# A two-layer attention and mixture-of-experts kernel: grouped column tiles, paired output products, shared reciprocals, contiguous weight pieces, more warming products

## The chip, the cores and the metric

One core of one Trainium2 chip runs the whole program. The metric is device time in microseconds (us) of that core for one execution; smaller is better. In this text PE is TensorE (matrix products), DVE is VectorE, ACT is ScalarE, POOL is GpSimd and SP is SyncE, which issues nearly all loads.

## What is computed

256 tokens of width 1024 go through two layers, all in float32. Cut to what matters:

```python
for i in range(2):
    xn = rms_norm(h, ln_mix[i])
    mix = nsa_attention(xn, ...) if i == 0 else moba_attention(xn, kb, vb, km, ...)
    h = h + mix                                   # 16 heads of 64, output projection 1024x1024
    h = h + hier_moe(rms_norm(h, ln_ffn[i]), ...) # 32 experts, 2 of them for each token
    gate = sigmoid(rms_norm(h, ln_ple[i]) @ ple_w_gate[i])
    h = h + gate * (p[i] @ ple_w_proj[i])

# nsa_attention: o = g0 * softmax(compressed) @ vc + g1 * softmax(selected) @ vs + g2 * softmax(window) @ vw
# hier_moe: hid = silu(x @ w_gate[e]) * (x @ w_up[e]); y = sum_e cw[e] * (hid @ w_down[e])
```

An expert has gate and up weights of 1024x128 each (1 MB together) and a down weight of 128x1024 (512 KB).

## The kernel before

Every product with a dense weight is made of three faster ones: a value is split into a high and a low half (ACT writes the high half, DVE the rest), and high times high, high times low and low times high are summed (L351 to L353, helper `mm3`). `Weights` (L109 to L132) loads a weight in pieces of two 128-row blocks and splits each block into a tile `wsp`; `xT` is the transposed input, loaded in between. The first such weight is B_c. Ahead of it `keep_warm` (L148, called at L599) lets PE multiply ones by ones eight times.

Attention runs over eight steps c, two heads each (`attend`, L500): scores of step c+1, the turn of step c (PE transposes the probabilities p0 and p1, L455 to L457), the softmax of step c+1, the products with the values (L473). In `softmax` (L416) DVE reduces, ACT takes the exponential with its sum, DVE takes the reciprocal (L434) and, in layer 0, multiplies it with the gate (L436), once for each head; then POOL scales the short tile p0 (L442, layer 0) and DVE the long tile p1 (L440). In layer 0 there are two branches (nbr is 2), in layer 1 one. The output projection is spread over the steps (`Out`, L529 to L557): the table ADD_AT names the step at which each piece j is multiplied, and DVE adds each result into the residual h (L540). Piece 3 comes in a tail. `Embedding.step` (L575) puts two further groups of products at steps 1 and 2.

In the mixture of experts, each expert takes up to 32 tokens. Four experts are one group j, and there are eight groups (L1287 to L1318). PE has four column tiles of 32 columns: products with `tile_position=(0, 32 * i)` go to tile i, for expert i of the group. `gate_up(j)` (L1170) makes eight steps k of four products of 128x256 (L1177); `hidden(j)` is ACT (L819, L821) and DVE (L822, L823) work on the result; `down(j)` (L1203) turns the hidden tile on PE (L1207), copies it (`hT`, L78), multiplies it with the down weights in two halves n of four products of 128x512 (L1221), splits each half (L340) and scatters the rows to their tokens (L1214). A ninth group holds one extra expert (`gate_up(8)`, L1183), whose weights POOL fetches by indirect transfers. `gate_up(j + 1)` and `hidden(j + 1)` are written ahead of `down(j)`. After the experts come L276 (transposes) and the products with ple_gate.

All loads stand on the queue of SP, in order, and go into a ring of SBUF, so a load starts when the tile that held its place is no longer used. A scheduler sets the order of the instructions of each engine from the code's order and its own estimates of when things are ready; it may put one product of a later group into a gap. Each engine then runs its list in order.

Of the kernel before, what the change touches and what calls it, by code (L numbers as in the profile page):

```python
# [18 lines left out]
P = 128  # L19
S = 256  # L20
# [19 lines left out]
def hybrid_kernel(ctx: ExitStack, tc: tile.TileContext, I: dict, out: bass.AP, dbg=None):  # L40
# [68 lines left out]
    class Weights:  # L109


        def __init__(self, w, g, turned=None):
            self.n, self.g, self.t, self.behind = w.shape[2], g, {}, []
# [302 lines left out]
    def softmax(c, nbr, raw, gates=None):  # L416

        a, i = divmod(c, 4)
        ws = []
        for b in range(2):  # L420
# [4 lines left out]
            mx = st("mx", [P, NT, nbr], bufs=4)  # L425
            sums = st("sums", [P, NT, nbr], bufs=4)
# [17 lines left out]
            ws.append((p0, p1))  # L444
# [55 lines left out]
    def attend(fill, after, nbr, qs, k1, k2, V, oT, gates=None, cmp=None):  # L500
# [3 lines left out]
        for c in range(8):  # L504
# [7 lines left out]
            if c < 7:  # L512
# [5 lines left out]
    ADD_AT = ((((3, 2), (3, 3)), ((4, 4), (4, 5)), ((7, 6), (7, 6))),  # L518
              (((3, 2), (3, 3)), ((5, 4), (5, 4)), ((6, 7), (7, 7))))

    class Out:
# [7 lines left out]
        def add(self, j, t, n):  # L529
            pt = pa([P, 512])  # L530
            for i in range(2):
                if self.l == 0:
                    w = self.w[j, i, n]
                    m = mm3(pt, [self.oT[j // 2][:, x, 2 * (j % 2) + i, t * P:(t + 1) * P] for x in range(2)],
                            [w[:, x] for x in range(2)], i == 0, i == 1)
                    continue
                m = nc.tensor.matmul(pt, self.oT[0][:, 2 * j + i, t * P:(t + 1) * P],  # L537
                                     self.raw[j][:, i, n * 512:(n + 1) * 512], start=(i == 0), stop=(i == 1))
# [10 lines left out]
        def step(self, c):  # L549
# [3 lines left out]
            for j in range(3):  # L553
                for t in range(NT):
                    for n in range(2):
                        if self.add_at[j][t][n] == c:
                            self.add(j, t, n)  # L557
# [3 lines left out]
    class Embedding:  # L561
# [13 lines left out]
        def step(self, c):  # L575
            if c in (1, 2):
                for n in range(2):
                    self.piece(c - 1, n)
# [20 lines left out]
    keep_warm(pts[0], 8)  # L599
# [226 lines left out]
    def moe(l, out_proj_tail, prefetch):  # L826
# [343 lines left out]
        def gate_up(j):  # L1170
            gu = pb([P, 3, P])
            xg = slots(j)
            if j < 8:
                wgu = wgus.pop(j)
# [335 lines left out]
```

## Time and profile before

| | |
|---|---|
| median of three timed runs | 553.49 us (550.83 to 555.04) |
| the profiled execution's own time | 546.59 us |
| its span in the trace | 544.8 us |
| PE busy | 518.6 us (95% of the span) |
| DVE, ACT, POOL busy | 341.0, 278.7, 51.9 us |
| loads | 147.16 MB, mean 270 GB/s |

Durations below are from the one profiled execution; 1.8 us of its time lie outside the span. A busy PE is not a PE at its peak: two products in two column tiles at once count like one that runs alone.

### The profile page before, as it was taken

The numbers are of one execution on the slowest core, as the hardware profiler recorded it, in microseconds if no ns is written. First come the engines' busy times: TensorE is split into PE (matmuls) and PEld (weight loads), VectorE is DVE, ScalarE is ACT, GpSimd is POOL, SyncE is SP. The second block draws the span as 40 slices with busy tenths as digits, with TensorE's granted clock in tenths as the row PEclk, the third lists the DMA queues.
The fourth block names the chain that finished last, engine by engine and source line by source line (L and its number), as shares of the span: only waits on it lengthen the run. The fifth ranks groups of instructions, "written<-read, shape, count | busy, mean of one in ns | idle before, by whom it ended". The sixth has DMA issues, their size and how long they took to land. (4 is left out here: it accounts for less than half of the span.)

```text
span 544.8 us, 10203 instructions
## 1 busy us (share of the span) xinstructions
PE 518.6 (95%) x3782; PEld 364.3 (67%) x3782; DVE 341.0 (63%) x1038; ACT 278.7 (51%) x650; POOL 51.9 (10%) x120
## 2 busy tenths in 40 slices
PE   6989999999998999999999999999997999899996
PEld 4968899578667766464448999755566655554386
DVE  4669978989966844323258975776748534142484
ACT  5729837976744242222349965763342413132491
POOL 5000402314330003100000000000000012000000
PEclk9999999999999899999999999999999999999999
DMA  8968650044779699999953678742555999999602
GB/s 288 426 244 306 225 225 2 1 155 152 300 284 333 217 426 416 410 417 416 400 231 117 220 275 374 295 149 98 192 206 221 385 420 418 417 417 401 247 1 77
DMA packets 32213, 147.16 MB, mean 270 GB/s; under 512 B 4000, under 2 KB 4272, under 8 KB 22304
## 3 DMA queue, kind: packets, MB, share of 16 engines
q1 hardware_dynamic: 31232, 144.39, 68.2%
q0 software_dynamic: 784, 2.05, 1.0%
q8 instruction: 31, 0.51, 0.4%
q14 instruction: 22, 0.18, 0.1%
q10 hardware_dynamic: 144, 0.04, 0.0%
HBM read 146.98 MB, written 1.05 MB: 272 GB/s over the span
## 5 line engine op out<-in xcount | busy, mean ns | idle before, releaser
L131 DVE SCALAR_TENSOR_TENSOR wsp<-raw,vec,wsp 128x512 fp32r<-128x512 f32 (+1 forms) x96 | 67.4, 747 | 5.5 <-ACT wsp L130 5.3
L130 ACT ACTIVATE wsp<-raw,vec 128x512 fp32r<-128x512 f32 (+1 forms) x96 | 62.6, 719 | 2.8 <-DMA raw<-in_w_c_dram 2.1
L1177 PE MATMUL pb<-wgu,X 128*32 128x256 f32 x768 | 56.9, 381 | 0.9 <-PEq L1295 0.6
L431 ACT ACTIVATE p<-p,mx 128x128 f32<-128x128 f32 (+1 forms) x96 | 42.5, 445 | 7.9 <-DVE mx L429 7.6
L819 ACT ACTIVATE p<-pb,srs 128x128 f32<-128x128 f32 x16 | 5.9, 367 | 77.0 <-PE pb L1177 70.0
L1177 PEld LDWEIGHTS pb<-wgu,X 128*32 128x32 f32 x768 | 29.9, 110 | 19.7 <-issue 3.4
L1221 PE MATMUL pb<-wd,hT 128*32 128x512 f32 x224 | 42.0, 595 | 0.7 <-issue 0.4
L351 PE MATMUL pa<-XA,wsp 128*128 128x256 f32 x128 | 38.3, 299 | 4.0 <-ACT wsp L130 3.3
L340 DVE TENSOR_TENSOR pta<-pb,p 128x512 fp32r<-128x512 f32 (+1 forms) x36 | 24.8, 690 | 24.4 <-ACT p L340 23.0
L353 PE MATMUL pa<-XA,wsp 128*128 128x256 f32 x128 | 37.2, 292 | 2.0 <-DVE wsp L131 2.0
L340 ACT CAST p<-pb 128x512 fp32r<-128x512 f32 (+1 forms) x36 | 21.0, 585 | 33.4 <-PE pb L1221 33.2
L352 PE MATMUL pa<-XB,wsp 128*128 128x256 f32 x128 | 37.3, 291 | 0.0
L822 DVE TENSOR_TENSOR p<-pb,ptb 128x128 f32<-128x128 f32 (+1 forms) x18 | 5.2, 289 | 43.3 <-ACT ptb L821 41.2
L442 POOL TENSOR_SCALAR p<-p,cf 128x128 f32<-128x128 f32 x32 | 25.6, 811 | 67.8 <-DVE cf L436 40.1
L460 ACT COPY pta<-pa 128x512 f32<-128x512 f32 (+1 forms) x32 | 14.6, 479 | 32.4 <-PE pa L456 32.4
L429 DVE CUSTOM_DVE_ANT_0 p<-pb,d_q 128x128 f32<-128x128 f32 (+1 forms) x96 | 29.4, 350 | 1.3 <-PE pa L455 0.9
L537 PE MATMUL pa<-wo,XH 128*128 128x512 f32 x64 | 29.4, 602 | 0.0
L351 PEld LDWEIGHTS pa<-XA,wsp 128*128 128x128 f32 x128 | 25.3, 198 | 5.9 <-ACT wsp L130 4.2
L1017 PE MATMUL pb<-rs,X 128*128 128x256 f32 (+1 forms) x192 | 27.1, 293 | 0.3 <-DVE X L1043 0.3
L1214 PE MATMUL pa<-p,rrow 128*128 128x512 f32 (+1 forms) x72 | 27.1, 424 | 0.2 <-ACT p L340 0.2
L1017 PEld LDWEIGHTS pb<-rs,X 128*128 128x128 f32 x192 | 24.3, 188 | 3.9 <-issue 1.2
L353 PEld LDWEIGHTS pa<-XA,wsp 128*128 128x128 f32 x128 | 25.1, 197 | 2.4 <-DVE wsp L131 2.4
(369 smaller groups left out, 1352.6 us busy)
## 6 DMA issues: line engine op xcount, KB each, us to landing
wgu<-in_moe_gu_dram SPq DMA_DIRECT2D x48, 1024.0 KB, 11.2
wd<-in_moe_w_down_dram SPq DMA_DIRECT2D x48, 512.0 KB, 9.8
wo<-in_w_out_dram SPq DMA_DIRECT2D x8, 1024.0 KB, 4.8
raw<-in_ple_gate_dram SPq DMA_DIRECT2D x16, 512.0 KB, 8.4
raw<-in_a_q_dram SPq DMA_DIRECT2D x8, 512.0 KB, 9.1
wd<-in_moe_w_down_dram SPq DMA_DIRECT2D x16, 256.0 KB, 7.8
XB<-in_moe_gu_dram SPq DMA_DIRECT2D x4, 1024.0 KB, 4.7
XA<-in_moe_gu_dram SPq DMA_DIRECT2D x4, 1024.0 KB, 4.9
```

What stands on the lines that cost most here:

```text
L130: nc.scalar.activation(hi, src, AF.Copy, scale=g)
L131: nc.vector.scalar_tensor_tensor(lo, src, g, hi.bitcast(F32), ALU.mult, ALU.subtract)
L340: return nc.scalar.copy(hi, src), eng.tensor_tensor(lo, src, hi.bitcast(F32), ALU.subtract)
L351: nc.tensor.matmul(o, a[0], b[0], start=first, stop=False)
L352: nc.tensor.matmul(o, a[0], b[1], start=False, stop=False)
L353: return nc.tensor.matmul(o, a[1], b[0], start=False, stop=last)
L429: nc.vector.tensor_tensor_reduce(pt_[:, br, :], st_[:, br, :], dt_, -SLOPE[hh], 3e38, ALU.add, ALU.min, accum_out=mx[:, t, br:br + 1])
L431: mark["exp", c] = nc.scalar.activation(pt_[:, br, :], pt_[:, br, :], AF.Exp, bias=mx[:, t, br:br + 1], scale=-1.0, accum_out=sums[:, t, b ...
L537: m = nc.tensor.matmul(pt, self.oT[0][:, 2 * j + i, t * P:(t + 1) * P], self.raw[j][:, i, n * 512:(n + 1) * 512], start=(i == 0), stop=(i ...
L1017: nc.tensor.matmul(pt, part_columns(x, t)[:, k, :], Gs[i][:, t, 0:e1], start=(t == x == 0), stop=(t == x == 1))
L1177: last_ = nc.tensor.matmul(gu[32 * i:32 * i + 32, 0:2], xg[:, k, 32 * i:32 * i + 32], wgu[i][k], start=(k == 0), stop=(k == NK - 1), tile_ ...
L1221: nc.tensor.matmul(ysp[32 * i:32 * i + 32, :], hT[:, 32 * i:32 * i + 32], wd[i][n], start=True, stop=True, tile_position=(0, 32 * i))
```

## The change

- `keep_warm` makes 18 products where it made 8.
- The pieces of weights and of xT lie contiguous in DRAM, where their rows lay apart. Bytes and transfers stay the same.
- In layer 0 the output products of pieces 0 and 1 are summed in one group of twelve products for each of four results, at steps 4 and 5, and added to h once; before, piece 0 was multiplied at step 3 and piece 1 at steps 4 and 5, with an addition each. There are 12 additions where there were 16.
- The second group of Embedding products moves from step 2 to step 3.
- Softmax takes one reciprocal (and in layer 0 one product with the gates) for both heads, and scales both heads' tiles behind it.
- In `gate_up` and `down` the experts of a group go from the last-loaded to the first, each product kept behind the one before it, so that the four column tiles stay together.

```diff
-                xT.append(load([P, 2, S], lambda t: [(t, turned[:, k:k + 2])], "xT"))
-            self.raw.append(load([P, 2, self.n], lambda t: [(t, w[:, k:k + 2])], "raw"))
+                xT.append(load([P, 2, S], lambda t: [(t, turned[k // 2])], "xT"))
+            self.raw.append(load([P, 2, self.n], lambda t: [(t, w[k // 2])], "raw"))
...
-            cf = st("cf", [P, NT, nbr], bufs=4)
-            nc.vector.reciprocal(cf, sums)
-            if gates is not None:
-                nc.vector.tensor_tensor(cf, cf, gates[:, :, 3 * hh + 1:3 * hh + 3], ALU.mult)
+            ws.append((p0, p1))
+        nc.vector.reciprocal(cfs, sums_)
+        if gates is not None:
+            g = gates.rearrange("p t (a b i j) -> p a b i t j", a=2, b=2, i=4)[:, a, :, i, :, 1:3]
+            nc.vector.tensor_tensor(cfs, cfs, g, ALU.mult)
+        for b in range(2):
+            p0, p1 = ws[b]
+            cf = cfs[:, b]
             for t, pt_ in enumerate((p0, p1)):
...
-    ADD_AT = ((((3, 2), (3, 3)), ((4, 4), (4, 5)), ((7, 6), (7, 6))),
-              (((3, 2), (3, 3)), ((5, 4), (5, 4)), ((6, 7), (7, 7))))
+    ADD_AT = ((((0, 1), ((4, 4), (5, 5))), (2, ((7, 6), (7, 6)))),
+              ((0, ((3, 2), (3, 3))), (1, ((5, 4), (5, 4))), (2, ((6, 7), (7, 7)))))
...
-            if c in (1, 2):
+            if c in (1, 3):
...
-    keep_warm(pts[0], 8)
+    keep_warm(pts[0], 18)
...
-                    for i in range(4):
-                        last_ = nc.tensor.matmul(gu[32 * i:32 * i + 32, 0:2], xg[:, k, 32 * i:32 * i + 32],
+                    for i in reversed(range(4)):
+                        with ExitStack() as es:
+                            if last_ is not None:
+                                es.enter_context(tc.issue_after(last_.ins))
+                            last_ = nc.tensor.matmul(gu[32 * i:32 * i + 32, 0:2], xg[:, k, 32 * i:32 * i + 32],
...
-                for i in range(m // 32):
-                    nc.tensor.matmul(ysp[32 * i:32 * i + 32, :], hT[:, 32 * i:32 * i + 32],
+                for i in reversed(range(m // 32)):
+                    with ExitStack() as es:
+                        if behind:
+                            es.enter_context(tc.issue_after(behind[0]))
+                        behind[:] = [nc.tensor.matmul(ysp[32 * i:32 * i + 32, :], hT[:, 32 * i:32 * i + 32],
```

What this does to PE's list, at three places of layer 0. Lines of the changed kernel are shifted: L1177 is L1189 there, L1183 is L1195, L1207 is L1219, L1214 is L1226, L1221 is L1238, L1017 is L1025. In a row, the tile written stands ahead of the arrow.

Place one, PE before, the scatter of the first group (pta and p are the low and high halves of its rows, wgu a gate and up weight of a later group):

```order
L1214 MATMUL pa_2265<-p_482_2508,rrow_2501 128x512
L1214 MATMUL pa_2267<-p_482_2508,rrow_2501 128x512
L1177 MATMUL pb_2545<-wgu_2365,X_467_2424 32x256
L1214 MATMUL pa_2265<-pta_2509,rrow_2501 128x512
L1214 MATMUL pa_2267<-pta_2509,rrow_2501 128x512
L1214 MATMUL pa_2266<-p_485_2517,rrow_2501 128x512
L1214 MATMUL pa_2266<-pta_2518,rrow_2501 128x512
L1214 MATMUL pa_2268<-p_485_2517,rrow_2501 128x512
```

The same place after the change:

```order
L1226 MATMUL pa_2227<-p_454_2470,rrow_2463 128x512
L1226 MATMUL pa_2229<-p_454_2470,rrow_2463 128x512
L1189 MATMUL pb_2507<-wgu_2333,X_439_2386 32x256
L1189 MATMUL pb_2507<-wgu_2331,X_439_2386 32x256
L1189 MATMUL pb_2507<-wgu_2329,X_439_2386 32x256
L1189 MATMUL pb_2507<-wgu_2327,X_439_2386 32x256
L1226 MATMUL pa_2227<-pta_2471,rrow_2463 128x512
L1226 MATMUL pa_2229<-pta_2471,rrow_2463 128x512
L1226 MATMUL pa_2228<-p_457_2479,rrow_2463 128x512
```

Before, one product of the next gate_up stands alone in the gap between the scatters of the high and the low half; after, all four column tiles of a step stand there.

Place two, PE before, from the end of gate_up(6) through down(5) (wd are down weights, hT the turned tile of group 5, pb_3068 the result of gate_up(6), which L1207 turns):

```order
L1177 MATMUL pb_3068<-wgu_2868,X_573_2934 32x256
L1221 MATMUL pb_3113<-wd_2870,hT_3109 32x512
L1221 MATMUL pb_3113<-wd_2872,hT_3109 32x512
L1221 MATMUL pb_3122<-wd_2870,hT_3109 32x512
L1221 MATMUL pb_3113<-wd_2874,hT_3109 32x512
L1221 MATMUL pb_3122<-wd_2872,hT_3109 32x512
L1221 MATMUL pb_3122<-wd_2874,hT_3109 32x512
L1207 MATMUL pb_3068<-ident,p_608_3103 128x128
L1221 MATMUL pb_3113<-wd_2876,hT_3109 32x512
L1221 MATMUL pb_3122<-wd_2876,hT_3109 32x512
L1214 MATMUL pa_2265<-p_612_3118,rrow_3111 128x512
```

And after (pb_3030 is the result of gate_up(6) here):

```order
L1189 MATMUL pb_3030<-wgu_2824,X_545_2896 32x256
L1219 MATMUL pb_3030<-ident,p_580_3065 128x128
L1238 MATMUL pb_3075<-wd_2838,hT_3071 32x512
L1238 MATMUL pb_3075<-wd_2836,hT_3071 32x512
L1238 MATMUL pb_3075<-wd_2834,hT_3071 32x512
L1238 MATMUL pb_3075<-wd_2832,hT_3071 32x512
L1238 MATMUL pb_3084<-wd_2838,hT_3071 32x512
L1238 MATMUL pb_3084<-wd_2836,hT_3071 32x512
L1238 MATMUL pb_3084<-wd_2834,hT_3071 32x512
L1238 MATMUL pb_3084<-wd_2832,hT_3071 32x512
L1226 MATMUL pa_2227<-p_584_3080,rrow_3073 128x512
```

Before, three experts' products for both halves come first, then the turn of group 6, then the fourth expert alone, for each half. After, the turn stands directly behind the last product of gate_up(6), and then come two full groups of four.

Place three, PE before, the turn of the extra expert (pb_2878, a tile of 32 columns; its L1183 products stand 32 L1177 products further up):

```order
L1177 MATMUL pb_2894<-wgu_2781,X_522_2685 32x256
L1207 MATMUL pb_2791<-ident,p_548_2826 128x128
L1207 MATMUL pb_2878<-ident,p_568_2889 128x32
L1017 MATMUL pb_2945<-rs_2682,X_374_2021 128x256
L1017 MATMUL pb_2945<-rs_2682,X_375_2022 128x256
```

And after (pb_2840 is the extra expert's tile):

```order
L1226 MATMUL pa_2230<-pta_2813,rrow_2796 128x512
L1195 MATMUL pb_2840<-X_491_2634,ptb_2387 32x256 x7
L1219 MATMUL pb_2753<-ident,p_520_2788 128x128
L1219 MATMUL pb_2840<-ident,p_540_2851 128x32
L1189 MATMUL pb_2856<-wgu_2743,X_494_2647 32x256
```

The turn of the extra expert's tile now follows its own products, with one other turn in between.

## Rows read from the trace of the kernel before

**Rows 1.** Windows: stretch, length, busy PE, PEld, DVE, ACT, POOL, clock, DMA share, GB/s:

```profile
85.00:170.00 85.00, 82.63 (x486) 60.74 (x485) 70.52 (x279) 59.12 (x188) 25.77 (x33) 1.00 0.44 166
187.50:282.00 94.50, 92.41 (x799) 50.16 (x799) 36.16 (x117) 26.88 (x60) 6.27 (x6) 1.00 0.99 398
436.00:514.00 78.00, 75.10 (x654) 38.92 (x654) 24.69 (x67) 19.82 (x44) 5.43 (x4) 1.00 1.00 404
```

**Rows 2.** Timeline of PE at the start: start, length, engine, line, operation, [idle before]:

```profile
1.14 3.60 PE L152 MATMUL pa<-ones 128*128 128x512 bf16 x8 [1.14 <-DVE eps_c L160]
8.00 0.58 PE L351 MATMUL pa<-XA,wsp 128*128 128x256 f32 x1 [3.26 <-ACT wsp L130]
```

**Rows 3.** Windows of PE alone, products of B_c: stretch, length, busy (count), clock:

```profile
8.00:13.40 5.40, 5.40 (x25) 1.00 1.04 418
13.40:22.00 8.60, 8.60 (x76) 1.00 1.05 430
```

**Rows 4.** Timeline of DVE behind B_c:

```profile
20.09 2.07 DVE L131 SCALAR_TENSOR_TENSOR wsp<-raw,vec,wsp 128x512 fp32r<-128x512 f32 x3
23.45 1.29 DVE L301 TENSOR_TENSOR p<-pa,rrow 128x512 f32<-128x512 f32 x2 [1.29 <-ACT rrow L295]
```

**Rows 5.** Groups of DVE, 85 to 170 us: count, busy us, mean ns, idle:

```profile
L540 DVE TENSOR_TENSOR XH<-XH,pa 128x512 f32<-128x512 f32 x15 | 9.9, 678 | 2.7 <-PE pa L353 2.7
...
L434 DVE RECIPROCAL cf<-sums 128x4 f32<-128x4 f32 x16 | 2.8, 172 | 1.5 <-ACT p L431 1.4
```

**Rows 6.** Timeline of POOL in the attention of layer 0:

```profile
107.84 3.21 POOL L442 TENSOR_SCALAR p<-p,cf 128x128 f32<-128x128 f32 x4 [6.80 <-DVE cf L436]
...
151.48 1.26 POOL L442 TENSOR_SCALAR p<-p,cf 128x128 f32<-128x128 f32 x2 [1.38 <-DVE cf L436]
```

**Rows 7.** Timeline of PE in the experts of layer 0:

```profile
199.88 0.62 PE L1177 MATMUL pb<-wgu,X 128*32 128x256 f32 x2
...
263.08 3.66 PE L1177 MATMUL pb<-wgu,X 128*32 128x256 f32 x64 [0.30 <-PEq L1295]
266.53 1.92 PE L1221 MATMUL pb<-wd,hT 128*32 128x512 f32 x12
...
268.38 0.33 PE L1207 MATMUL pb<-ident,p 128*128 128x128 f32 x1
268.64 1.90 PE L1221 MATMUL pb<-wd,hT 128*32 128x512 f32 x4
...
271.14 1.04 PE L1221 MATMUL pb<-wd,hT 128*32 128x512 f32 x2
...
273.69 1.90 PE L1221 MATMUL pb<-wd,hT 128*32 128x512 f32 x10
```

**Rows 8.** Timeline of ACT behind gate_up(7) of layer 0:

```profile
266.91 0.37 ACT L819 ACTIVATE p<-pb,srs 128x128 f32<-128x128 f32 x1 [3.73 <-PE pb L1177]
```

**Rows 9.** Timeline of DVE behind gate_up(7) of layer 0:

```profile
267.89 0.29 DVE L823 TENSOR_TENSOR p<-p,p 128x128 f32<-128x128 f32 x1
268.75 0.29 DVE L78 COPY hT<-pb 128x128 f32<-128x128 f32 x1 [0.56 <-PE pb L1207]
```

**Rows 10.** Timeline of PE in the experts of layer 1:

```profile
465.13 0.59 PE L1183 MATMUL pb<-X,ptb 128*32 128x256 f32 x2 [1.78 <-DMA X<-in_moe_gu_dram,rowi]
...
502.23 1.88 PE L1221 MATMUL pb<-wd,hT 128*32 128x512 f32 x8
504.50 1.05 PE L1221 MATMUL pb<-wd,hT 128*32 128x512 f32 x4 [0.39 <-issue]
...
505.75 1.90 PE L1221 MATMUL pb<-wd,hT 128*32 128x512 f32 x4
...
508.24 1.04 PE L1221 MATMUL pb<-wd,hT 128*32 128x512 f32 x2
...
510.80 1.92 PE L1221 MATMUL pb<-wd,hT 128*32 128x512 f32 x14
```

**Rows 11.** DMA issues at 491.9 to 492.2 us: count, KB, us to landing:

```profile
wd<-in_moe_w_down_dram SPq DMA_DIRECT2D x1, 256.0 KB, 7.9
```

More of the change, by code (lines that the diff above doesn't have):

```diff
@@ L112, in __init__ @@
         def __init__(self, w, g, turned=None):
-            self.n, self.g, self.t, self.behind = w.shape[2], g, {}, []
+            self.n, self.g, self.t, self.behind = w.shape[3], g, {}, []
             self.raw = []
@@ L419, in softmax @@
         ws = []
+        mxs = st("mx", [P, 2, NT, nbr], bufs=2)
+        sums_ = st("sums", [P, 2, NT, nbr], bufs=2)
+        cfs = st("cf", [P, 2, NT, nbr], bufs=2)
         for b in range(2):
@@ L424, in softmax @@
             p0 = wt("p0", [P, nbr, P], bufs=4)
-            mx = st("mx", [P, NT, nbr], bufs=4)
-            sums = st("sums", [P, NT, nbr], bufs=4)
+            mx, sums = mxs[:, b], sums_[:, b]
             for t, (pt_, st_, dt_) in enumerate(((p0, s0, d_q0), (p1, s1, d_q1))):
@@ L527, in __init__, with add @@
                 self.raw.append(load([P, 2, D], lambda t: [(t, I["w_out"][l, j])], "wo"))
-        def add(self, j, t, n):
+        def add(self, js, t, n):
             pt = pa([P, 512])
[L531 to L538, printed above, removed]
+            js = (js,) if isinstance(js, int) else js
+            for j in js:
+                for i in range(2):
+                    first, last = j == js[0] and i == 0, j == js[-1] and i == 1
+                    if self.l == 0:
+                        w = self.w[j, i, n]
+                        m = mm3(pt, [self.oT[j // 2][:, x, 2 * (j % 2) + i, t * P:(t + 1) * P] for x in range(2)],
+                                [w[:, x] for x in range(2)], first, last)
+                        continue
+                    m = nc.tensor.matmul(pt, self.oT[0][:, 2 * j + i, t * P:(t + 1) * P],
+                                         self.raw[j][:, i, n * 512:(n + 1) * 512], start=first, stop=last)
             hs = hh[0][:, t, n * 512:(n + 1) * 512]
@@ L552, in step @@
                     self.split(c - 2)
-            for j in range(3):
+            for js, at in self.add_at:
                 for t in range(NT):
                     for n in range(2):
-                        if self.add_at[j][t][n] == c:
-                            self.add(j, t, n)
+                        if at[t][n] == c:
+                            self.add(js, t, n)
     pj = cp.tile([P, NT, D], F32, name="pj")
@@ L575, in step @@
         def step(self, c):
-            if c in (1, 2):
+            if c in (1, 3):
                 for n in range(2):
-                    self.piece(c - 1, n)
+                    self.piece(c // 2, n)
     gm0 = g_mix[:, 0, :]
@@ L1217, in down @@
             ysxs = []
+            behind = []
             for n in range(2):
                 ysp = pb([P, 512])
-                for i in range(m // 32):
-                    nc.tensor.matmul(ysp[32 * i:32 * i + 32, :], hT[:, 32 * i:32 * i + 32],
-                                     wd[i][n], start=True, stop=True,
-                                     tile_position=(0, 32 * i))
+                for i in reversed(range(m // 32)):
[3 more added lines that the diff above has]
+                        behind[:] = [nc.tensor.matmul(ysp[32 * i:32 * i + 32, :], hT[:, 32 * i:32 * i + 32],
+                                                      wd[i][n], start=True, stop=True,
+                                                      tile_position=(0, 32 * i)).ins]
                 yhi = wt("p1", [P, 512], F32R, bufs=4)
```

19 lines of the change are left out of this document (11 added, 8 removed).

## Prediction, made before the changed kernel was run

> **What bounds the kernel now.** I read the windows first, stage by stage. In the three stages that the change touches most, PE is busy 82.63 of 85.00 us (attention of layer 0), 92.41 of 94.50 (experts of layer 0) and 75.10 of 78.00 (experts of layer 1) [rows 1]. So PE's own list sets the time, and little can be had by removing waits. What can be had is work on PE that is done one column tile at a time. The second thing to see in these rows is the share of the DMA engines: 0.44 in the attention, but 0.99 and 1.00 in the two stages of experts. A faster PE runs into its loads there. Then I read the timelines of PE within those stages, the ACT and DVE rows that feed PE, and the order of the changed kernel.
>
> **Warming products and contiguous pieces.** Eight warming products take 3.60 us, 0.45 each, and end at 4.7; PE then waits 3.26 us for the first split weight and starts B_c at 8.00 [rows 2]. Its first 25 products take 5.40 us, 0.216 each, the next 76 take 8.60, 0.113 each [rows 3]. [...] PE had been running without a break since 8.00 when its products became fast. With 18 warming products it runs without a break from 1.14. If the rise falls within them, they end between 4.7 + 10 x 0.225 = 7.0 and 9.2, and I expect an end near 8, when the weight is there. All of B_c then runs at the fast spacing and could end 25 x 0.103 = 2.6 us earlier. But DVE writes low halves until 22.16, and its next step waits 1.29 us for the row copy that hangs on PE [rows 4]; only that much can come forward. Term: -1.3. On the other side, if the rise does not come in time, 18 products of 0.45 end at 9.24, so B_c starts 1.2 late. The bounds are -1.3 and +1.2; I take -1.3, since PE would have been busy for some 7 us by then, longer than the 5.40 at the slow spacing before.
>
> [...]
>
> Contiguous pieces: the strided pieces of B_c and what follows already come at 418 and 430 GB/s [rows 3], no less than the contiguous expert weights at 398 and 404 [rows 1]. I cost this at nothing; 0 to -0.5.
>
> **Attention of layer 0.** DVE loses 8 reciprocals of 172 ns (1.4 us), as many gate products, and 4 additions of 678 ns (2.7 us) [rows 5]. PE's products are the same in number. DVE is busy 70.52 of 85 us, so its relief is worth at most the time in which PE is not busy, 85.00 - 82.63 = 2.4 us [rows 1]. Against this, POOL now scales four short tiles behind the shared reciprocal, where it could do the first two while the second head was still being summed. Two took 1.26 us, four in a row 3.21 [rows 6]: the last tile is ready 1.26 to 1.95 us later, eight times. PE's turn stands behind it, and behind the turn the value products and the next scores. For the turns of steps 5 and 6 PE has more to do meanwhile than before, the twelve-product groups. For those of steps 2 and 3 it has less, as piece 0 has left step 3, so I let two turns pay 1.26 each: +2.5, against -2.4. Term: 0; bounds -2.4 and +15.6 (8 x 1.95).
>
> In layer 1 eight reciprocals go from DVE, which PE does not wait for, and POOL has no part: 0. Embedding's move changes PE's filling only, and is in the bounds above.
>
> **Experts of layer 0.** A step of gate_up, four column tiles at once, is (266.53 - 263.08)/8 = 0.43 us. Before, a single product stands in the gap between two scatters (the one at 199.88) [rows 7]; its step is then done by three column tiles later, and costs 0.43 again. The order has five such places in each layer, four alone and one cut by another group. Afterwards a whole step stands in the gap or none is cut (place one of the order): 5 x 0.43 = -2.15.
>
> A step of down is half of 1.85 us, the time from 266.53 to 268.38 for three experts in two halves [rows 7], so 0.92. In down(5) the fourth expert alone takes two more steps; the group needs two in all, which saves 1.84. But at place two the turn now stands straight behind gate_up(6), and its input comes by way of ACT and DVE: behind gate_up(7), whose successor started at 266.53, ACT starts at 266.91, DVE ends at 268.18, and the turn starts at 268.38 [rows 7 to 9]. That is 1.85 us, which the three experts' products used to fill. Nothing fills it now: net 0. In down(6) and down(7) I count nine steps before (2 at 266.53, 2 at 268.64, 1 at 271.14 and two more of that kind, 2 at 273.69) and five after (two; two for a half cut in pairs; one): -3.7. The turn of down(7) is followed by its products at once, so PE waits for the copy hT, from 268.38 to 269.04 [rows 7, 9]: +0.7. At place three the extra expert's turn stands behind its own products and pays the chain of 1.85, which 32 products covered before: +1.85.
>
> Sum: -2.15 + 0 - 3.7 + 0.7 + 1.85 = -3.3. Bounds: -7.0 if the two bare turns cost nothing, -1 if the grouped products gain only in down(6) and down(7) and the gap then stalls.
>
> **Experts of layer 1.** Again -2.15 and, at down(5), 0. The extra expert's turn is covered here. Down(6) and down(7) go from seven steps (two for the rows at 502.23 and 504.50, two at 505.75, one at 508.24, two at 510.80) to four: -2.8 [rows 10]. PE waits 1.78 us at 465.13 for the extra expert's gathered rows [rows 10]; their gather is now issued ahead of the other one, but PE comes 1.7 us (4 x 0.43) earlier, so I take about half, -0.8. That makes -5.7. The loads limit it: a load of down(7) issued at 492 lands 7.9 us later, at 499.9 [rows 11]; the last load of down(6) is the one before it, by 256 KB at 404 GB/s (0.65 us), an estimate of 499.3. PE asked for it at 502.23 and now asks 2.95 earlier, at 499.3. So there is no more slack, and with the last-loaded expert first the whole group waits for that load. I charge 0.4. Term: -5.3; bounds -7.5 and -2.9.
>
> **Sum.** -1.3 + 0 + 0 - 3.3 + 0 - 5.3 = -9.9 against the profiled execution's 546.59: 536.7. The median of the runs shown, 553.49, is 1.26% above that execution; by the same ratio the forecast is 536.7 x 1.0126 = 543.5.
>
> **Rivals.**
> - Loads end the experts' stages. For it: shares of 0.99 and 1.00 [rows 1] and the slack just used up in layer 1. Against it: PE idles only 2 to 3 us in each stage now, so the loads were ahead. If they were just in time in both layers, a little over a third of the gain would stay, -3 in all: 550.5.
> - More is gained: the turns at places two and three find their input ready, because the loads or the scatter ahead of them delay the products anyway, and DVE's relief removes the attention's waits. -9.9 - 3.7 - 2.4 = -16: 537.3. Against it: the order puts nothing else there.
> - Slower: POOL's four scalings stand on the path of every turn. For it: a turn can't begin before them, and turns follow one another closely. The price is 8 x 1.95 = 15.6 instead of nothing: 546.59 + 5.7 = 552.3, or 559.3 by the ratio. It decides from 9.9/8 = 1.24 us of uncovered delay for each turn, which is about the uncontended price. Against it: four or more output products stand ahead of most turns.
> - The grouping does nothing, because the column tiles of one group overlap whichever products stand between them. Against it: the single product at 199.88 and the pair at 271.14 each hold PE for a whole step [rows 7]. Then only the start is left, and the bare turns cost 3.7: 546.59 - 1.3 + 3.7 = 549.0, by the ratio 555.9.
>
> **Chances.** Forecast 0.58, of loads 0.15, of more gain 0.14, of POOL 0.07, of no grouping 0.06. The likeliest one's own range is 539 to 549. The range of 8 in 10 reaches from 535, past the case of more gain, to 554, past that of the loads. A measurement here tells differences of about 1% (5.5 us) from none. Faster by that, below 548.0: nearly all of the forecast's case, all of more gain and a little of the loads, 0.74. Within it: 0.20. Slower: most of POOL's, 0.06.
>
> **What would show it.** Right: PE products of gate_up only in fours; a wait of some 1.8 us at the turn behind gate_up(6) in both layers and at the extra expert's in layer 0; the products of B_c at 0.113 from the first one; down(6) and down(7) in five and four steps; in layer 1 PE waiting for wd. Wrong: turns in the attention of layer 0 that wait over 1.2 us each; the last warming product past 8.0; the experts' stages as long as 94.5 and 78.0 us. The forecast as a whole is wrong if the stages of experts together shrink by less than 5 us or the attention grows by more than 4.

## The result, and the profile after

| | before | after |
|---|---|---|
| median of 17 runs, side by side | 550.83 us | 543.56 us (540.55 to 546.08) |
| ratio after / before | | 0.991 [0.988, 0.994] |
| profiled execution's own time | 546.59 us | 544.75 us |
| span, mean granted clock | 544.8 us, 0.995 | 542.9 us, 0.978 |

The changed kernel takes 7.3 us less by the medians and about 5 us (0.9%) less by the ratio, which leaves out the five executions of before that are more than 1.5% above its fastest. The forecast of 543.5 us is met to a tenth of a microsecond, but by luck: two errors cancel, which the stages show. As a share, 1.8% less was forecast (536.7 for 546.59) and 0.9% was measured.

One caution for every comparison below: the profiled execution of before was one of its best. Sixteen of its 17 runs go from 545 to 556 us (one took 733). Its mean granted clock, the share of full speed that the trace records, was 0.995; the executions of before beside the experiments go from 0.999 down to 0.980. The 17 of after have clocks from 0.978 to 0.991, and the profiled one is among the lowest.

The table gives the length of each stage on PE: from the first product of one kind to the first, or last, of the next. "Undone" is the experiment e5, which is after without its two edits of the attention and without Embedding's move. Each column is one execution.

| stage on PE, us | before | after | forecast | measured | undone |
|---|---|---|---|---|---|
| start to first scores | 81.36 | 77.94 | -1.3 | -3.4 | 78.50 |
| attention layer 0 (first scores to last turn) | 79.31 | 87.28 | 0 | **+8.0** | 79.31 |
| last turn to gate_up(0), layer 0 | 23.17 | 23.19 | 0 | 0 | 25.05 |
| experts layer 0 (gate_up(0) to last scatter) | 97.08 | 91.69 | -3.3 | -5.4 | 92.02 |
| from there to the scores of layer 1 | 58.69 | 58.36 | 0 | -0.3 | 58.52 |
| attention layer 1 | 56.55 | 57.52 | 0 | +1.0 | 56.54 |
| last turn to gate_up(0), layer 1 | 21.65 | 23.85 | 0 | +2.2 | 22.61 |
| experts layer 1 | 97.75 | 92.94 | -5.3 | -4.8 | 91.84 |
| last scatter to the end | 29.21 | 30.16 | 0 | +1.0 | 30.19 |
| sum | 544.8 | 542.9 | -9.9 | -1.8 | 534.6 |

The windows of [rows 1] have fixed ends, and the stages move against them. So here are the windows of each kernel over its own attention of layer 0, experts of layer 0 and experts of layer 1 (the columns as in [rows 1]), of before:

```profile
81.36:160.67 79.31, 76.94 (x463) 57.39 (x462) 69.90 (x282) 57.80 (x185) 25.77 (x33) 1.00 0.38 146
183.84:280.91 97.07, 95.67 (x863) 52.21 (x863) 37.99 (x138) 26.63 (x60) 6.27 (x6) 1.00 0.98 396
417.80:515.55 97.75, 94.54 (x859) 51.82 (x859) 37.51 (x137) 27.27 (x63) 5.43 (x4) 1.00 0.94 384
```

and of after:

```profile
77.94:165.22 87.28, 82.64 (x464) 60.39 (x462) 67.58 (x262) 57.09 (x185) 22.03 (x33) 0.94 0.31 115
188.41:280.10 91.69, 87.11 (x859) 49.53 (x859) 37.67 (x138) 27.97 (x62) 5.28 (x6) 1.00 0.99 401
419.83:512.76 92.93, 87.91 (x855) 49.70 (x855) 36.68 (x136) 27.57 (x63) 4.71 (x4) 0.98 0.96 390
```

DVE does 20 operations less in the attention, as intended, and is busy for 2.3 us less. PE gained nothing by it: for the same products it is busy for 82.64 us, where it was 76.94, it is idle for 4.6 us, where it was 2.4, and its clock is 0.94. In the experts PE is busy for 8.6 us less in layer 0 and 6.6 in layer 1, again for the same products (a few records are missing), and idle for 3.2 and 1.8 us more.

The start, PE timeline of after, to be held beside [rows 2], and its windows beside [rows 3]:

```profile
1.14 5.58 PE L152 MATMUL pa<-ones 128*128 128x512 bf16 x18 [1.14 <-DVE eps_c L160]
6.37 0.47 PE L351 MATMUL pa<-XA,wsp 128*128 128x256 f32 x1
```

```profile
8.00:13.40 5.40, 5.40 (x47) 1.00 1.02 413
13.40:22.00 8.60, 8.60 (x75) 1.00 1.05 434
```

47 products stand in the stretch that held 25. B_c runs at the fast spacing from its first product (5.40 us for the 47, 0.115 each, where the 25 had 0.216), and PE doesn't wait between the last warming product and B_c.

[Rows 3] begin at 8.00, when the first pieces have landed. Ahead of that the loads (the last column, GB/s) were slower before:

```profile
2.00:4.00 2.00, 2.00 (x6) 1.00 0.83 189
4.00:6.00 2.00, 0.74 (x2) 1.00 0.87 239
```

than they are after:

```profile
2.00:4.00 2.00, 2.00 (x6) 1.00 0.92 323
4.00:6.00 2.00, 2.00 (x10) 1.00 1.02 381
```

The attention of layer 0 in after: the group of waits for POOL's scaling, then two of its rows in PE's timeline, then three windows of PE alone:

```profile
PE pa L460 <- POOL p L448: 3.2, 4, 1.7
```

```profile
108.45 0.33 PE L460 MATMUL pa<-ident,p 128*128 128x128 f32 x1 [1.71 <-POOL p L448]
...
123.08 0.33 PE L460 MATMUL pa<-ident,p 128*128 128x128 f32 x1 [0.79 <-POOL p L448]
```

```profile
98.00:108.00 10.00, 8.30 (x53) 1.00 0.00 1
108.00:118.00 10.00, 8.98 (x40) 0.60 0.01 2
118.00:128.00 10.00, 8.61 (x34) 0.88 0.44 160
```

The two uncovered turns are where the prediction put them, at steps 2 and 3. What it didn't foresee stands in the last columns: after the first wait the granted clock is at 0.50 for 10.2 us (110.1 to 120.3, a mean of 0.60 and 0.88 in the windows).

Experts of layer 0 in after, PE timeline, to be held beside [rows 7]:

```profile
204.46 0.64 PE L1189 MATMUL pb<-wgu,X 128*32 128x256 f32 x8
...
239.94 0.21 PE L1219 MATMUL pb<-ident,p 32*128 32x32 f32 x1 [1.16 <-DVE p L831]
...
261.68 0.30 PE L1219 MATMUL pb<-ident,p 128*128 128x128 f32 x1 [1.54 <-DVE p L831]
261.91 1.92 PE L1238 MATMUL pb<-wd,hT 128*32 128x512 f32 x16
...
269.90 1.93 PE L1238 MATMUL pb<-wd,hT 128*32 128x512 f32 x16
271.75 0.33 PE L1219 MATMUL pb<-ident,p 128*128 128x128 f32 x1
272.46 1.05 PE L1238 MATMUL pb<-wd,hT 128*32 128x512 f32 x4 [0.38 <-DVE hT L78]
...
276.66 1.06 PE L1238 MATMUL pb<-wd,hT 128*32 128x512 f32 x8
```

A product of gate_up or down is two records, so a step of four products is x8. The lone products are gone: gate_up stands in whole steps in the gaps (x8 at 204.46). The row with x16, all four experts for both halves of down, takes 1.92 us, as long as the one with x12, three experts, did before. The two bare turns wait 1.16 and 1.54 us, the copy hT 0.38. Another turn, at 220.54, waits 0.80 us, which no turn did before.

Experts of layer 1 in after, to be held beside [rows 10]:

```profile
464.92 0.62 PE L1195 MATMUL pb<-X,ptb 128*32 128x256 f32 x2
...
492.48 0.30 PE L1219 MATMUL pb<-ident,p 128*128 128x128 f32 x1 [1.49 <-DVE p L831]
...
502.62 1.08 PE L1189 MATMUL pb<-wgu,X 128*32 128x256 f32 x8 [2.16 <-issue]
503.42 3.21 PE L1238 MATMUL pb<-wd,hT 128*32 128x512 f32 x16
...
508.91 1.92 PE L1238 MATMUL pb<-wd,hT 128*32 128x512 f32 x16
```

The wait for the gathered rows has gone altogether (464.92). A new one of 2.16 us, for nothing that the profile shows, cuts gate_up(7), and behind it a group of down takes 3.21 us where the next takes 1.92: the granted clock is at 0.50 there for 3.4 us (502.6 to 506.0).

### The profile page after: what moved, and what is told of

Same layout as the page of the kernel before. It is cut to its first block, busy times and chain, and to the rows that moved or that the text cites. A ratio compares the mean times of both kernels' runs of the same rounds, so it can differ in the third digit from the quotient of the medians.

```text
span 542.9 us, 10150 instructions
## 1 busy us (share of the span) xinstructions
PE 513.1 (95%) x3792; PEld 364.9 (67%) x3792; DVE 336.9 (62%) x1010; ACT 278.4 (51%) x650; POOL 47.0 (9%) x120
## 5 line engine op out<-in xcount | busy, mean ns | idle before, releaser
L1189 PE MATMUL pb<-wgu,X 128*32 128x256 f32 x768 | 53.1, 384 | 2.8 <-issue 2.2
L1189 PEld LDWEIGHTS pb<-wgu,X 128*32 128x32 f32 x768 | 27.4, 110 | 21.3 <-issue 5.8
L353 PE MATMUL pa<-XA,wsp 128*128 128x256 f32 x128 | 36.4, 284 | 2.1 <-DVE wsp L131 2.1
L351 PE MATMUL pa<-XA,wsp 128*128 128x256 f32 x128 | 37.4, 292 | 0.8 <-DVE rs L301 0.8
L1238 PE MATMUL pb<-wd,hT 128*32 128x512 f32 x224 | 29.4, 620 | 0.4 <-DVE hT L78 0.4
L448 POOL TENSOR_SCALAR p<-p,cf 128x128 f32<-128x128 f32 x32 | 21.9, 698 | 79.0 <-DVE cf L439 34.5
L1226 PE MATMUL pa<-p,rrow 128*128 128x512 f32 (+1 forms) x72 | 26.9, 421 | 0.0
L1025 PE MATMUL pb<-rs,X 128*128 128x256 f32 (+1 forms) x192 | 26.5, 292 | 0.0
L1226 PE MATMUL pa<-pta,rrow 128*128 128x512 f32 (+1 forms) x72 | 26.4, 416 | 0.0
L1025 PEld LDWEIGHTS pb<-rs,X 128*128 128x128 f32 x192 | 24.2, 188 | 2.6 <-issue 2.5
L353 PEld LDWEIGHTS pa<-XA,wsp 128*128 128x128 f32 x128 | 24.1, 189 | 2.5 <-DVE wsp L131 2.5
```

The lines of the kernel that those rows point to most:

```text
L351: nc.tensor.matmul(o, a[0], b[0], start=first, stop=False)
L353: return nc.tensor.matmul(o, a[1], b[0], start=False, stop=last)
L1025: nc.tensor.matmul(pt, part_columns(x, t)[:, k, :], Gs[i][:, t, 0:e1], start=(t == x == 0), stop=(t == x == 1))
L1189: last_ = nc.tensor.matmul(gu[32 * i:32 * i + 32, 0:2], xg[:, k, 32 * i:32 * i + 32], wgu[i][k], start=(k == 0), stop=(k == NK - 1), tile_ ...
L1226: nc.tensor.matmul(y[t][n], gt[0:m, t * P:(t + 1) * P], ysx[x][0:m], start=(first and x == 0), stop=(final and x == 1))
L1238: behind[:] = [nc.tensor.matmul(ysp[32 * i:32 * i + 32, :], hT[:, 32 * i:32 * i + 32], wd[i][n], start=True, stop=True, tile_position=(0, ...
```

## The experiments

Unless it says otherwise, each is the changed kernel with one edit, and "stage" is the attention of layer 0 as in the table. Ratios are to before, run beside it.

**e1: the pairing of output products undone.** ADD_AT and Out as before; Embedding's move and the shared softmax stay.

```diff
-    ADD_AT = ((((0, 1), ((4, 4), (5, 5))), (2, ((7, 6), (7, 6)))),
+    ADD_AT = ((((3, 2), (3, 3)), ((4, 4), (4, 5)), ((7, 6), (7, 6))),
```

> The changed kernel with the table and the loop of the output projection as before (piece 0 at step 3, sixteen additions in layer 0). In the changed kernel the stretch from the first scores to the last turn of layer 0 took 87.3 us against 79.3 before, and the clock stood at half for 10.2 us in it. Theory A (pieces 0 and 1 left PE without products ahead of the turns of steps 2 and 3; the rest follows from that): the half-clock stretch goes and the stage comes to 79 to 81 us, the whole to 535 to 538 in the profile. Theory B (POOL's four scalings behind the shared reciprocal are late at every turn): the stage stays at 84 us or more.

Measured: 537.61 us, ratio 0.981 [0.968, 0.993]; stage 83.17 at a clock of 1.00. The stretch at a clock of 0.50 is gone, as theory A has it, but the stage lies between the two theories.

**e2: the shared softmax undone.** One reciprocal and one product with the gates for each head; pairing and Embedding's move stay.

```diff
-        nc.vector.reciprocal(cfs, sums_)
+            cf = st("cf", [P, NT, nbr], bufs=4)
+            nc.vector.reciprocal(cf, sums)
```

> The changed kernel with the softmax as before (a reciprocal and a gate product for each head, POOL scaling the first head early). Theory A: the stage of 87.3 us shrinks by at most 2 us, and the half-clock stretch stays. Theory B: it comes back to 79 to 81 us, PE waits nowhere for POOL.

Measured: 538.45, ratio 0.980 [0.969, 0.990]; stage 83.22. One wait of it and the clock behind it, from the PE timeline and the windows (121 to 125 us):

```profile
119.71 0.44 PE L766 MATMUL pb<-ident,sq 128*128 128x128 f32 x2 [2.13 <-DVE sq L761]
```

```profile
121.00:125.00 4.00, 4.00 (x16) 0.57 0.78 270
```

Either undoing gives back half of the 8 us, which is neither theory's number. So neither edit alone is the cause.

**e5: both undone, and Embedding back at steps 1 and 2.** Run twice, in two sessions.

```diff
-            if c in (1, 3):
+            if c in (1, 2):
```

> The changed kernel with both attention edits undone (table, sixteen additions, a softmax for each head, Embedding at steps 1 and 2); warming, contiguous pieces and grouped experts stay. Undoing either one alone gave back 7.4 to 8.5 us of the changed kernel's span. If each of the two is needed for the loss, undoing both gives no more than undoing one: 533 to 536 in the span. If their losses had added up, it would be 528 or less.

> The kernel with grouped experts, contiguous pieces and 18 warming products, but the attention of before, run again beside the next two, to compare with them on one chip. It had a span of 534.6 us in its profile and 531.4 to 536.3 us in four runs; the half-clock stretches in its profiled run were 10.2 us in the router of layer 0 and 3.4 in that of layer 1. If these stretches fall differently from run to run, the span moves by up to half their length, 2 to 5 us, with the same order of instructions.

Measured: 533.95, ratio 0.973 [0.967, 0.980], and 536.48, ratio 0.981 [0.974, 0.988]. The stage is 79.31 both times, the 79.31 of before. The three edits of the attention together cost all of the 8.0 us. The span of 534.6 is the one that was expected if each of the two edits is needed for the loss, but the stage says that the losses add up. The span hides it: both profiled executions have 10.2 us at a clock of 0.50 in the router of layer 0 and 3.4 in that of layer 1 (a mean of 0.985 over the span), and e1 has none (1.000). The other executions of this kernel differ, with times from 531.40 us at a mean clock of 0.998 to 538.14 at 0.981.

**e12: e5 with Embedding's second group at step 3 again.** It moves one part alone.

```diff
-            if c in (1, 2):
+            if c in (1, 3):
```

> The kernel whose attention is that of before (label e5_attn) with one edit put back: the second group of Embedding products at step 3 instead of step 2. Its attention stage, first scores to last turn, was 79.3 us; with the shared reciprocal and Embedding at step 3 it was 83.2, with the paired output products and Embedding at step 3 also 83.2, with all three 87.3. Embedding's move was in both of the 83.2. If it alone costs the 3.9 us (PE runs out of products ahead of the turn of step 3), the stage is about 83 here. If the shared reciprocal and the pairing cost 3.9 each, it stays at 79 to 80.

Measured: 536.16, ratio 0.978 [0.970, 0.986]. Stage 79.72, so the move costs 0.4 in layer 0. In layer 1 the attention takes 57.53 with the move (this run, e1, e2, after) and 56.54 without it (before, e5): the +1.0 there is this move. The shared softmax then adds 83.17 - 79.72 = 3.5, the pairing 83.22 - 79.72 = 3.5, and both 7.6.

Where the softmax's share begins is seen at step 2. DVE of e12, the two heads' reciprocals:

```profile
103.62 0.18 DVE L434 RECIPROCAL cf<-sums 128x4 f32<-128x4 f32 x1
...
105.53 0.17 DVE L434 RECIPROCAL cf<-sums 128x4 f32<-128x4 f32 x1
```

DVE of after, the shared one, and ACT's last sum for it:

```profile
105.84 0.42 DVE L431 CUSTOM_DVE_ANT_0 p<-pb,d_q 128x256 f32<-128x256 f32 x1 [1.68 <-PE pb L410]
...
107.11 0.20 DVE L436 RECIPROCAL cf<-sums 128x8 f32<-128x8 f32 x1
```

```profile
105.39 0.19 ACT L433 ACTIVATION_READ_ACCUMULATOR p<-p,mx 128x1 f32 x1
```

The sums are complete at 105.58, but the reciprocal comes at 107.11. It stands in DVE's list behind reductions of the next step's scores, which wait 1.68 us for PE. So the shared reciprocal is late not only by the second head, as the prediction had it, but by 1.5 us of list order on top. The first head's tiles, which had their own reciprocal at 103.62 in e12, now wait for it too. In PE's timeline of e1 the turns of steps 2 and 3 start 2.2 us later than in e12 and that of step 7 4.0 us later (the first scores 0.2); the granted clock of e1 is 1.00 in the whole stage. The loss isn't idle time there, as PE's windows over the stage show, for e1 and then for e12:

```profile
78.34:161.51 83.17, 80.51 (x464) 1.00 0.37 139
```

```profile
78.13:157.86 79.73, 76.83 (x463) 1.00 0.38 146
```

For the same products at the same clock PE is busy 3.7 us longer, while it is idle for 2.7 us in place of 2.9. Most of this is in the value products. Those of the two heads go to the two halves of PE's columns, and side by side their times overlap: in e12 56 records of 394 ns, 22.1 us in sum, hold PE for 10.0. In e1 five of them stand alone in the list, in e12 three, in before one (a product is two records here too). Their records are as long, but together they hold PE for more time, in e12 and then in e1:

```profile
L473 PE MATMUL pa<-pta,X 128*64 128x256 f32 x56 | 10.0, 394 | 1.2 <-ACT pta L460 1.2
```

```profile
L478 PE MATMUL pa<-pta,X 128*64 128x256 f32 x56 | 11.5, 397 | 0.7 <-ACT pta L465 0.7
```

With those of 128x128 it is 2.2 us more in all, of the 3.4 by which e1's stage is longer. Where the rest comes from is not shown.

**e6: six products of ones ahead of the turns of steps 2 and 3.** They do no useful work.

```diff
+                if c in (2, 3):
+                    keep_warm(pa([P, 2, S]), 6)
                 pts = turn(nbr, ws)
```

> The changed kernel with six products of ones by ones put on PE ahead of the turns of steps 2 and 3 of layer 0; nothing is left out. They do no useful work. If the half-clock stretch of 10.2 us in the attention is a follow-up of PE's idle time there, it goes, and the stretch from the first scores to the last turn falls from 87.3 to 82 to 84 us although the waits for POOL remain. If the loss is the waits alone, the stage stays at 87 us or grows by the 2 to 3 us that the products take.

Measured: 542.14, ratio 0.987 [0.981, 0.993]; stage 83.94. Two windows of PE, for the 0.60 and 0.88 of after:

```profile
108.00:118.00 10.00, 9.04 (x50) 1.00 0.00 0
118.00:128.00 10.00, 8.52 (x50) 1.00 0.62 211
```

The clock of 0.50 is gone from the stage. Twelve useless products, 2.9 us of PE in two blocks, make it 3.3 us shorter. So the clock costs some 3.3 of the 8.0; half of the 10.2 us at 0.50, 5.1, is the most that it can be.

PE's list in this stage is the same in three other kernels below. In e3 and e7, with 10.2 us at a clock of 0.50 in two pieces, it takes 87.85 and 88.06 us; in e4, with 3.4 us, 85.53. So the 8.0 is one execution's number. In e4 the clock goes to 0.50 only at 122.8, behind the turn of step 3:

```profile
121.46 0.33 PE L460 MATMUL pa<-ident,p 128*128 128x128 f32 x1 [2.45 <-POOL p L448]
```

From the turn of step 2 to this one are 11.68 us, as in e6 (11.66), and 14.63 in after. The 2.95 us between them are the price of the clock there, without any filling. The clock of 0.50 also hides a wait: at 1.00 PE comes earlier to the turn of step 3 and waits 2.45 us for POOL, where it waited 0.79.

**e3: the experts' loops of before.**

```diff
-                    for i in reversed(range(4)):
+                    for i in range(4):
```

(In gate_up and in down, and without the chain that keeps each product behind the one before.)

> The changed kernel with the experts' loops as before (expert 0 first, products free to be put apart). If the grouping is what shortened the experts' stages, the stretch from the first gate_up to the last scatter is longer again by 5 us in layer 0 (97 instead of 91.7) and by 4.5 to 5 in layer 1 (97.7 instead of 92.9), and the whole is 553 to 555 in the profile. If the loads had set these stages, less than 2 us in each.

Measured: 551.42, ratio 1.002 [0.997, 1.006]: without the grouping the change gains nothing at all. The two stages of experts take 94.19 + 99.73 = 193.9 us, with the grouping 91.69 + 92.94 = 184.6. It is worth 9.3 us, and it also makes the stretch from the last scatter to the end 1.0 longer (29.15 here, 30.1 to 30.2 in all grouped kernels); why stays open. The split is not the expected one: layer 0 loses 2.5 us and layer 1 6.8. The list is not quite that of before (down(6) of layer 0 stands whole here), and the execution has a wait of 2.15 us for "issue" in layer 1.

**e4: eight warming products; e7: the strided pieces of before.** Two edits, in two kernels.

```diff
-    keep_warm(pts[0], 18)
+    keep_warm(pts[0], 8)
```

```diff
-                self.raw.append(load([P, 2, self.n], lambda t: [(t, w[k // 2])], "raw"))
+                self.raw.append(load([P, 2, self.n], lambda t: [(t, w[:, k:k + 2])], "raw"))
```

> The changed kernel with 8 warming products. If the clock of the first products is the gain at the start, B_c runs slowly for some 25 products again and the first scores come 2.5 to 3.4 us later; if the earlier start of B_c (6.4 instead of 8.0) comes from the contiguous loads, the first product still starts by 6.6, and the first scores come 1 to 1.8 us later.

> The changed kernel with the weights' and xT's rows apart in DRAM as before. With 8 warming products but contiguous pieces the first real product could start at 6.0, before at 8.0. If the contiguous pieces bring the first loads earlier, the first real product starts at 7.8 to 8.2 here and the first scores come 1 to 2 us later than in the changed kernel; if they bring nothing, within 0.5 us of it.

Measured: e4 544.34, ratio 0.989 [0.978, 1.001]; e7 545.48, ratio 0.994 [0.988, 1.000]. PE's first rows, of e4:

```profile
1.14 3.60 PE L152 MATMUL pa<-ones 128*128 128x512 bf16 x8 [1.14 <-DVE eps_c L160]
6.02 0.58 PE L351 MATMUL pa<-XA,wsp 128*128 128x256 f32 x1 [1.28 <-ACT wsp L130]
```

and of e7:

```profile
1.14 6.63 PE L152 MATMUL pa<-ones 128*128 128x512 bf16 x18 [1.14 <-DVE eps_c L160]
8.36 0.39 PE L351 MATMUL pa<-XA,wsp 128*128 128x256 f32 x1 [0.59 <-ACT wsp L130]
```

With before and after they make a square of first scores: 81.36 (8, strided), 80.45 (18, strided), 79.28 (8, contiguous), 77.94 (18, contiguous). More warming is worth 0.9 and 1.3 us, contiguous pieces 2.1 and 2.5. With the same eight warming products, the first split weight is there at 6.02 in place of 8.00. The loads between 2 and 4 us come at 322 GB/s in e4 and at 190 in e7, so their rate goes with the layout and not with the warming.

**e8: e1 with 14 warming products.**

```diff
-    keep_warm(pts[0], 18)
+    keep_warm(pts[0], 14)
```

> The changed kernel with the table of before, and 14 warming products instead of 18, which moves every later PE instruction 8 places up. The kernel with 18 lost 2.3 us to a wait of PE in gate_up(7) of layer 1 that no engine and no load explains, and at that moment a transfer of 16 KB on the instruction queue was under way; with 8 the wait was in layer 0. If it comes from where a block of instructions ends behind the branch, it moves or shrinks with 14. If it comes from the loads of the experts, it stays at 2 us in gate_up(7) of layer 1.

Measured: 540.51, ratio 0.986 [0.979, 0.994]; e1 had 0.981 [0.968, 0.993], so no difference that this shows. The wait for "issue" in gate_up(7) of layer 1 stays, at the same product of the list and with 2.15 us for 2.31. By the expectation that speaks for the loads and against the end of a block of instructions, but it is one shift by four products:

```profile
497.20 0.64 PE L1186 MATMUL pb<-wgu,X 128*32 128x256 f32 x8 [2.15 <-issue]
```

**e9: e5, and the two bare turns kept behind the products of the previous group.** The turn of group 6 and that of the extra expert.

```diff
-            nc.tensor.transpose(gu[:, 2, 0:m], hid, ident[0:m, 0:m])
+            with ExitStack() as es:
+                if prods and j in (6, 8):
+                    es.enter_context(tc.issue_after(prods[0]))
+                nc.tensor.transpose(gu[:, 2, 0:m], hid, ident[0:m, 0:m])
...
+                prods[:] = behind
```

> The same kernel with the turn of group 6 and of the extra expert kept behind the products of the group before. If the bare turns are what was lost in the experts' stages, the waits of 1.5 us behind gate_up(6) and of 1.2 at the extra expert go in layer 0, and 1.5 in layer 1; the stretch from the first gate_up to the last scatter is 2 to 2.7 us shorter in layer 0 and 1 to 1.5 in layer 1. If the loads take it back, PE waits for wd or wgu instead and the stages stay within 0.5 us.

Measured: 530.97, ratio 0.971 [0.964, 0.978]. Experts of layer 0 90.48 (e5 92.02), of layer 1 90.37 (91.84): 1.5 us in each. For layer 0 more was expected (2 to 2.7), but the wait of 1.16 us at the extra expert's turn, which after has, isn't there in e5. PE's rows for the two turns in layer 0, with no wait ahead of them:

```profile
245.13 0.24 PE L1215 MATMUL pb<-ident,p 32*128 32x32 f32 x1
...
257.10 0.27 PE L1215 MATMUL pb<-ident,p 128*128 128x128 f32 x1
```

**e11: e9, and six products of ones more in each router,** between the ordering of the slots and the gathers of the tokens. They do no useful work.

```diff
-            order(0)
+            i = order(0)
+        with tc.issue_after(i.ins):
+            i = keep_warm(pg[0], 6)
```

> The kernel with the moved turns, and six more products of ones by ones between the ranking product and the first gathering products of each layer's router, where PE waited 1.5 us. They do no useful work. If the half-clock stretches at the routers follow that wait, they go in both layers, and the span is 2 to 5 us under that of the kernel with moved turns alone, about 528 to 530. If the later wait of 0.7 us or the small products of the router cause them, they stay.

Measured: 527.92 (526.95 to 528.31), ratio 0.966 [0.962, 0.970]: 3.4% below before and, by the two ratios, 2.5% below the change as it was made. PE's windows in the stretches of [rows 1] (this kernel's stages end earlier, so the counts don't compare), and its two waits for loads in the experts of layer 1:

```profile
85.00:170.00 85.00, 82.64 (x488) 1.00 0.47 179
187.50:282.00 94.50, 91.17 (x785) 1.00 1.00 403
436.00:514.00 78.00, 74.02 (x585) 1.00 0.85 345
```

```profile
482.29 3.66 PE L1184 MATMUL pb<-wgu,X 128*32 128x256 f32 x64 [0.62 <-DMA wgu<-in_moe_gu_dram]
...
487.81 1.92 PE L1237 MATMUL pb<-wd,hT 128*32 128x512 f32 x16 [1.85 <-DMA wd<-in_moe_w_down_dram]
```

The granted clock stays at 1.00 until 523.9 (a mean of 0.998 over the span). The routers (first transposes to gate_up(0)) take 14.87 and 15.27 us where e9 had 17.72 and 17.70, each with 6.8 to 10.2 us at a clock of 0.50 (174.0 to 184.2 and 406.0 to 412.8). Now PE waits for its loads in layer 1, 2.5 us in all: here is the bound of which the first rival spoke. It begins to show in e9, with 0.80 us for a gate and up weight (at 488.8), and in e4, with 0.38 for a down weight (at 504.17).

## Why the prediction was right, and where it was wrong

**The time hit by luck, two steps missed.** The sum gave 536.7 for the profiled execution; it took 544.75, 8.05 more. The failed step is the one for "Attention of layer 0", "Term: 0", which measured +8.0. The prediction itself named an attention that grows by more than 4 us as a sign that the forecast as a whole is wrong, and so it is, though the time fits. The other failed step is "by the same ratio the forecast is 536.7 x 1.0126 = 543.5": the profiled execution of after stands at its median (544.75 beside 543.56, a ratio of 0.998), so this step put 6.8 us on the sum that weren't there. The ratio 1.0126 came from three runs; by the median of 17 it would be 1.008. And the extra of before's median over its profile was not a fixed share of any kernel. It goes with the clock: beside the experiments before took 544.41 us at a mean clock of 0.999 and 553.17 at 0.981. The profiled execution had 0.995, and the forecast carried this over.

**Attention of layer 0: the place right, the price wrong.** The forecast let two turns, of steps 2 and 3, pay 1.26 each; PE waits for POOL at these two turns and at no other, 3.2 us in all, and 4.9 in e4, where the clock is 1.00 between them. But "+2.5, against -2.4" fails twice. DVE's relief returned nothing that shows: the stage is longer in every kernel that has any of it (e1, e2), and 79.31 in the two that have none (before, e5). And behind the wait the clock stands at 0.50 for 10.2 us, which e6 prices at 3.3. The bound of +15.6 held; the rival of POOL's four scalings "on the path of every turn" did not come true at every turn, and its name of the culprit is half of it, as the pairing without the shared softmax costs the same 3.5. Of that, e2 shows a wait of 2.1 us and 3.4 us at a clock of 0.50; the rest is open.

**Embedding and layer 1.** "Embedding's move changes PE's filling only, and is in the bounds" failed as a term for layer 1, where it costs 1.0 (e12).

**Start: right in kind, too small.** PE goes from the warming products to B_c without a wait, and all of B_c runs at the fast spacing: 0.9 to 1.3 us for the forecast's 1.3. The step that failed is the one on contiguous pieces, "I cost this at nothing". It compared rates from 8.00 on, 418 against 398 GB/s, and those are indeed unchanged (413 and 434). What counts is the time before, in which the first pieces come: there the rate rose from 189 and 239 GB/s to 323 and 381, and the first split weight came 2 us earlier.

With the same eight products before it, B_c got fast at 13.4 us in before (0.216 us a product, then 0.113) and at 10.2 in e4 (19 products in 4.18 us, then 34 in 3.80), having run without a break since 8.00 and 6.02. With 18 products from 1.14 on, the spacing of the warming products themselves fell in all eleven profiled executions, between 4.2 and 6.7 us: in after from 0.427 to 0.216 us, so that the 18 take 5.58 us, and in the second run of e5 so late that they take 6.81. The forecast's 0.225 for a fast one, half of its 0.45, was the author's estimate; after has 0.216. What sets the moment is not shown.

**Experts of layer 0: -3.3 forecast, -5.4 measured.** The mechanism is confirmed by e3: gate_up stands only in fours, and down(6) and down(7) take five steps (four in layer 1), as predicted. PE's busy time fell by 8.6 us for a forecast of 7.7, and its idle time grew by 3.2 for 4.4. The mis-sized terms are the waits: the extra expert's bare turn cost 1.16 for 1.85, the turn behind gate_up(6) 1.54 for 1.85, hT 0.38 for 0.7, together 1.3 less. The wait of 0.80 at 220.54 no term had.

**Experts of layer 1: -5.3 forecast, -4.8 measured.** The gather's wait went wholly (-1.78 for -0.8), the bare turn cost 1.49 for 1.85, no load was late (0 for +0.4), and the products, without the stretch at 0.50, took 7.9 us less for a forecast of 6.8. But the unforeseen wait of 2.16, 1.3 us for the clock of 0.50 behind it (3.21 - 1.92) and a wait of 0.74 ahead of another turn (at 452.2) took back more. "PE waiting for wd", a sign of being right, did not come: the loads "were ahead", as argued against that rival, until e9 and e11.

**Given back elsewhere.** The router of layer 1 took 17.47 us for 15.27, with the clock at 0.50 from 413.9 on for 6.8 us. In before, e1, e2 and e3 it took 15.3 at a clock of 1.00, so this is not a cost of the edits there. Why the clock fell here and not in those is open. With +1.0 at the end, these make 3.2 us that no term had.

## What to carry to other kernels

Price a wait on PE by what it can do to the clock as well: here waits of 1.5 to 2.2 us were followed by 3.4 to 10.2 us at a granted clock of 0.50, though not in every kernel, and a few useless products in the gap paid for themselves. Work shared between two heads or pieces (one reciprocal, one addition) relieved an engine that didn't bound here, while it held the first head back to the second, and to whatever the scheduler put in between. Keep the column tiles of a group together, and see in the order what the grouping has laid bare; read a rate in the stretch in which it is needed; before adding a profile's distance to a median, see at which clock that execution ran.

## What the runs showed of the hardware beyond what was expected

- Pieces that lie contiguous made the first weight usable about 2 us earlier (first product 6.02 for 8.00 with 8 warming products). Between 2 and 4 us they came at 322 and 323 GB/s (e4, after), the strided ones at 189 and 190 (before, e7); from 8 us on both came at 413 to 434 GB/s (before, after).
- Stretches at a granted clock of 0.50 came in the middle of the kernel, of 3.4, 6.8 or 10.2 us, in the attention, the routers and the experts, and not at the same place in two kernels whose list there is the same: e1 and e8, which differ by four warming products at the start, take 14.87 and 17.31 us in the router of layer 0. In after each begins at or behind a wait of PE of 1.5 to 2.2 us (which ends at 108.45, 181.77, 411.93 and 502.62; the clock is at 0.50 from 110.1, 181.7, 413.9 and 502.6). But such a wait is not enough: e1 has waits of 1.5 to 2.3 us too (178.02, 406.64 and 495.01) and stays at a clock of 1.00 from 5.2 to 534.2.
- In the last group of experts PE stops for 2.1 to 2.5 us on "issue" in ten of the kernels (in layer 0 in e4, in layer 1 in the others), and for 1.6 in e9. In after it ends 2.4 us after a transfer of 16 KB begins on the queue that the profile names instruction (500.18, and PE goes on at 502.62), while the loads keep the DMA engines at a share of 1.03 (498 to 502); the 0.39 of before [rows 10] ends 2.6 us after such a transfer too (501.95). That the one causes the other no run separated; e11 doesn't show the wait, and why its place differs stays open.
